# Splitting GpSimd's first load by partitions in a diagonal prefix-sum kernel

## The chip, the cores and the metric

The kernel runs on one core of a Trainium2 chip. The metric is the device time of one execution in microseconds; shown are the median and the extremes of three runs. One further execution was taken with the hardware profiler; all views of the profile are of that one.

## The reference

The input is four float32 matrices of 4224 x 4224. For each the two-dimensional prefix sum is formed, its diagonal is taken, and the diagonal is summed up again:

```python
def setup_inputs():
    B, H, W = 4, 4224, 4224
    return {"x": np.random.randn(B, H, W).astype(np.float32)}

def reference(x):
    ps = np.cumsum(np.cumsum(x, axis=1), axis=2)
    diag = np.diagonal(ps, axis1=1, axis2=2)
    return np.cumsum(diag, axis=1).astype(np.float32)
```

So the output has 4 x 4224 numbers, and every element of the input has to be read once: 285 MB.

## The kernel before

**Tiling.** A matrix is worked through in strips of 768 rows: partition p holds six consecutive rows of it, so a strip tile is 128 x 6 x 4224 in bfloat16 (6336 KB written, twice that read). Five such strips and one of 384 rows (three per partition) make a matrix; the last matrix (b = 3) ends in smaller pieces. The loads change float32 to bfloat16 on the way, which the loads issued from GpSimd do here. There are three strip buffers, reused in turn.

**What a strip needs.** `add_up` sums the columns right of the diagonal block with matmuls by the selector `sel` (lines 219 and 226), cuts the diagonal block with a mask (`tensor_mul` at 361, `tensor_sub` at 362), sums rows left of it on ACT (`act_sum`, 261) and on DVE (`row_sums`, 266). At the end of each matrix a few small operations on 11 x 384 numbers make its part of the output.

**Order.** The schedule is manual: each engine works in program order. DMAs go out on two queues: SyncE's (SP, line 78 and 83, and the results at the end), shown in the profile as q1 hardware_dynamic, and GpSimd's, shown as q0 software_dynamic, which carries all other loads. Both feed the same sixteen DMA engines. A load into a strip buffer (`load_rows`, line 71) waits for the buffer's earlier readers, and stands in GpSimd's order among GpSimd's other work.

**The start.** These steps stand ahead of everything else:

- line 78, SP: `opening`, row 0 of each partition's six in strip 0, in float32 (2112 KB), into the first strip buffer, used as float32 space
- line 83, SP: `head`, 128 x 2 x 528 numbers of the last matrix in float32 (528 KB)
- line 87, GpSimd: rows 1 and 2 of strip 0 (2112 KB written), then rows 3 to 5 (3168 KB), into the second buffer
- line 71, GpSimd: strip 1 (6336 KB) into the third buffer
- line 89, ACT: casts `opening` into row 0 of strip 0

Then, in program order: DVE sums `head` (line 93), makes `sel` (96, 97) and the first mask (102); GpSimd cuts the masks (103 and on) and makes some small constants up to line 208. GpSimd's next instruction after these is the load of strip 2 (line 71) into the buffer that `opening` held. Its wait is for SP's opening load and ACT's cast.

Of the kernel before, what the change touches and what calls it, by code (L numbers as in the profile page):

```python
# [17 lines left out]
def kernel(  # L18
# [14 lines left out]
    nc = tc.nc  # L33
# [3 lines left out]
    P = 128  # L37
    F = 3
    F2 = 2 * F
# [26 lines left out]
    def strip_tile():  # L66
        return strips.tile([P, F2, N], BF16, name="strip")

    def load_rows(o, b, r0):
        f = o.shape[1]  # L70
        nc.gpsimd.dma_start(  # L71
            out=o, in_=x[b, r0 : r0 + f * P, :].rearrange("(p f) w -> p f w", f=f)
        )


    src_0 = x[0, : F2 * P, :].rearrange("(p f) w -> p f w", f=F2)
# [6 lines left out]
    nc.sync.dma_start(out=head, in_=src_a[:, :, N - HC : N])  # L83

    prefetched = [strip_tile(), strip_tile()]
    for f0, f1 in ((1, F), (F, F2)):
        nc.gpsimd.dma_start(out=prefetched[0][:, f0:f1], in_=src_0[:, f0:f1])
    load_rows(prefetched[1], 0, F2 * P)
    nc.scalar.copy(out=prefetched[0][:, 0], in_=opening)  # L89

# [8 lines left out]
    def upper_mask(f):  # L99
# [22 lines left out]
        out=um1,  # L122
        in_=um1,
# [10 lines left out]
        out=ident,  # L134
        in_=ident,
# [32 lines left out]
    def between_groups(name, turned):  # L168
# [27 lines left out]
        out=weights,  # L196
        in_=weights,
# [12 lines left out]
        out=steps, in_=steps, scalar=2, op=ALU.arith_shift_right  # L210
# [112 lines left out]
    for b in range(B):  # L323
# [86 lines left out]
        for h in range(2):  # L410
# [3 lines left out]
                out=r6[ps, k : k + 2 * ns : 2, :], in_=a6[ps, :, :, 1]  # L414
# [27 lines left out]
        if not whole:  # L442
# [9 lines left out]
            for sb, c0, c1 in (  # L452
# [8 lines left out]
                    out=part_b[:, sb, c0:c1],  # L461
                    in_=x[b, r0 : r0 + R, :TB].rearrange("r (k c) -> r k c", k=4)[
                        :, :, c0:c1
                    ],
# [29 lines left out]
        for i, (to, src) in enumerate(((c1, d), (c2, c1))):  # L494
            nc.vector.tensor_tensor_scan(  # L495
                out=to,
# [52 lines left out]
        for i in (1, 0):  # L549
# [3 lines left out]
            out=out[b, T0 : T0 + M0].unsqueeze(0), in_=yl[:, :M0]  # L553
        )
        nc.sync.dma_start(
            out=out[:LB, :].rearrange("b (g i) -> g b i", i=GW), in_=whole_sums
        )
        nc.sync.dma_start(
            out=out[b, :T0].rearrange("(g i) -> g i", i=GW), in_=last_sums[1:NG]
# [3 lines left out]
        for i in (1, 0):  # L563
# [8 lines left out]
            out=out[b, T0 + M0 : T0 + E0].unsqueeze(0), in_=yl[:, M0:E0]  # L572
# [35 lines left out]
```

## Time and profile before

| | us |
|---|---|
| median of three runs | 667.44 (667.38 to 667.51) |
| the profiled execution's own time | 667.36 |
| its span, from first to last instruction | 665.6 |
| PE busy | 214.9 |
| DVE busy | 379.8 |
| ACT busy | 139.1 |
| POOL (GpSimd) busy | 31.6 |
| first GpSimd load: from issue to landing | 17.2 |
| opening load (SP): from issue to landing | 12.3 |
| head load (SP): from issue to landing | 38.9 |
| a six-row strip load: from issue to landing, median of 18 | 65.5 |

The span is cut into 40 equal slices for some rows; a digit is a busy share in tenths, and 9 stands for 90% or more. In the rows of DMA queues the three numbers are packets, MB (counted as written) and the share of the time of sixteen engines that the packets took; when packets overlap in the records, the share passes 100%. The chain of waits follows the work that ended last back from the end, and prints, for each piece, start and duration in us. In the timeline each row has start, duration, engine, line, operation, and in brackets how long the engine was idle before and what ended that.

### The profile page before, as it was taken

The page shows a single profiled execution, that of the slowest core. Times are in us where ns is not written, and L with a number is a line of the kernel's source. Part 1 is how long each engine was busy: PE and PEld are TensorE (multiplying, and loading weights), DVE is VectorE, ACT ScalarE, POOL GpSimd, SP SyncE. Part 2 cuts the span into 40 slices and gives each one's busy share as a digit, 9 for nine tenths or more (in the row PEclk, how much of TensorE's full clock was granted, in tenths as well). Part 3 has the DMA queues.
Part 4 walks back from the last instruction along what each step waited for, and adds up shares of the span by engine and source line. Part 5 has one row for each costly group of instructions (what it writes and reads, how often), then busy time and mean ns, then how long its engine had stood idle before and what let it go on. Part 6 is the DMA issues. An engine that isn't in the chain of part 4 may idle for free.

```text
span 665.6 us, 2565 instructions
## 1 busy us (share of the span) xinstructions
PE 214.9 (32%) x979; PEld 97.5 (15%) x980; DVE 379.8 (57%) x176; ACT 139.1 (21%) x220; POOL 31.6 (5%) x60
## 2 busy tenths in 40 slices
PE   0044522403118143140311723404031354340468
PEld 0021211100003021010000311201000121120123
DVE  0045938476946173756794526456589433362866
ACT  2001121406300103040630020304063002030433
POOL 1014000000000000000000000000000000001000
PEclk9996757556558585665655858667555595775768
DMA  9999999999999999999999999999999999999998
GB/s 256 223 227 219 219 219 219 213 207 215 219 219 218 219 220 219 218 218 213 210 218 219 217 216 219 219 219 214 218 213 215 220 213 219 218 219 218 218 204 162
DMA packets 7810, 144.31 MB, mean 217 GB/s; under 512 B 714, under 2 KB 1014, under 8 KB 2166
## 3 DMA queue, kind: packets, MB, share of 16 engines
q0 software_dynamic: 7312, 141.39, 99.2%
q1 hardware_dynamic: 486, 2.77, 1.2%
q8 instruction: 7, 0.11, 0.1%
q14 instruction: 5, 0.04, 0.0%
HBM read 285.47 MB, written 0.07 MB: 429 GB/s over the span
## 4 chain that ended last, share of the span: by engine, by line
DVE 47%; another core or an unknown queue 30%; DMA 18%; POOL 2%; issue 1%; PE 1%; DVEq 0%; SPq 0%; POOLq 0%
DVE acc L266 25%; DMA strip<-in_x_dram 12%; DVE rowed L266 7%; DVE mu L361 7%; DVE strip L362 7%; DMA head<-in_x_dram 6%; POOL um L103 1%; PE d L219 1%; DVE um L102 1%; DVE c L495 0%; DVE whole_sums L495 0%; POOL strip L460 0%; DVE pu L266 0%; DVE whole_sums L287 0%
## 5 line engine op out<-in xcount | busy, mean ns | idle before, releaser
L261 ACT ACTIVATE dump<-strip 128x416 bf16<-128x416 bf16 (+6 forms) x108 | 123.6, 1145 | 505.4 <-DMA strip<-in_x_dram 502.7
L266 DVE TENSOR_REDUCE acc<-strip 128x6 f32<-128x4608 bf16 (+6 forms) x23 | 195.9, 8518 | 0.4
L361 DVE TENSOR_TENSOR mu<-strip,um 128x4608 bf16<-128x4608 bf16 (+1 forms) x24 | 52.4, 2183 | 221.1 <-DMA strip<-in_x_dram 221.0
L226 PEld LDWEIGHTS <-sel 128*11 128x11 bf16 x643 | 66.5, 103 | 435.8 <-issue 406.1
L219 PE MATMUL d<-strip,sel 128*11 128x384 bf16 x90 | 36.5, 406 | 281.0 <-DMA strip<-in_x_dram 239.4
L226 PE MATMUL d<-strip,sel 128*11 128x384 bf16 x441 | 113.6, 400 | 0.0
L219 PE MATMUL d<-mu,sel 128*11 128x384 bf16 x43 | 16.6, 386 | 117.6 <-DVE mu L361 117.5
L362 DVE TENSOR_TENSOR strip<-strip,mu 128x4608 bf16<-128x4608 bf16 (+1 forms) x24 | 52.4, 2183 | 1.0
L266 DVE TENSOR_REDUCE rowed<-strip 128x384 f32<-128x2304 bf16 x12 | 48.8, 4067 | 0.0
L226 PE MATMUL d<-mu,sel 128*11 128x384 bf16 x200 | 48.0, 377 | 0.0
L71 POOL DMA_DIRECT2D strip<-in_x_dram x23 | 15.7, 681 | 500.7 <-DVE acc L266 268.2
L93 DVE TENSOR_REDUCE hs<-head 128x2 f32<-128x1056 f32 x1 | 1.3, 1253 | 40.2 <-DMA head<-in_x_dram 40.2
L219 PEld LDWEIGHTS <-sel 128*11 128x11 bf16 x134 | 13.6, 102 | 60.4 <-DVE sel L97 41.6
L219 PE MATMUL d<-rowed,sel_f 128*11 128x384 f32 x24 | 12.6, 616 | 25.3 <-DVE rowed L266 25.3
L261 ACT ACTIVATION_READ_ACCUMULATOR dump<-strip 128x1 f32 x108 | 20.1, 186 | 0.0
L219 PE MATMUL d<-ident,rows 128*11 128x128 f32 x24 | 5.2, 378 | 16.8 <-DVE rows L422 16.8
L219 PE MATMUL fold<-um,ident_h 128*128 128x512 bf16 x27 | 8.1, 475 | 0.3 <-issue 0.3
L103 POOL TENSOR_SCALAR_AFFINE_SELECT um<-um 128x4608 bf16<-128x4608 bf16 (+1 forms) x2 | 5.2, 2610 | 43.4 <-DVE um L102 43.4
L89 ACT CAST strip<-strip 128x4224 bf16<-128x4224 f32 x1 | 3.7, 3711 | 11.1 <-DMA strip<-in_x_dram 11.1
L219 PEld LDWEIGHTS d<-rowed,sel_f 128*11 128x11 f32 x24 | 1.4, 93 | 30.1 <-DVE rowed L266 30.0
L266 DVE TENSOR_REDUCE pu<-d 11x1 f32<-11x384 f32 x4 | 2.2, 546 | 6.2 <-PE d L219 6.2
L102 DVE MEMSET um<- 128x4608 bf16 (+1 forms) x2 | 4.9, 2458 | 1.1 <-issue 1.1
(108 smaller groups left out, 77.3 us busy)
## 6 DMA issues: line engine op xcount, KB each, us to landing
strip<-in_x_dram POOLq DMA_DIRECT2D x18, 6336.0 KB, 65.5
strip<-in_x_dram POOLq DMA_DIRECT2D x6, 3168.0 KB, 55.8
strip<-in_x_dram SPq DMA_DIRECT2D x1, 2112.0 KB, 12.3
strip<-in_x_dram POOLq DMA_DIRECT2D x1, 2112.0 KB, 17.2
strip<-in_x_dram POOLq DMA_DIRECT2D x1, 1080.0 KB, 49.9
strip<-in_x_dram POOLq DMA_DIRECT2D x1, 768.0 KB, 52.9
strip<-in_x_dram POOLq DMA_DIRECT2D x3, 256.0 KB, 54.1
head<-in_x_dram SPq DMA_DIRECT2D x1, 528.0 KB, 38.9
```

The lines of the kernel that those rows point to most:

```text
L71: nc.gpsimd.dma_start(out=o, in_=x[b, r0 : r0 + f * P, :].rearrange("(p f) w -> p f w", f=f))
L89: nc.scalar.copy(out=prefetched[0][:, 0], in_=opening)
L93: nc.vector.reduce_sum(out=hs[:, 0:2], in_=head, axis=AX.X)
L102: nc.vector.memset(um, 1.0)
L103: nc.gpsimd.affine_select(out=um, in_=um, compare_op=ALU.is_gt, fill=0.0, base=0, pattern=[[-1, f], [1, f * P]], channel_multiplier=-f,)
L219: nc.tensor.matmul(o, lhsT=lhsT, rhs=rhs, start=start, stop=False, skip_group_check=True)
L226: te.add_instruction(mybir.InstMatmult(start_tensor_calc=False, stop_tensor_calc=False, tile_position=(0, 0), tile_size=(P, P if lhsT.shap ...
L261: nc.scalar.activation(out=dump[:, :w], in_=src, func=ACT.Copy, accum_out=acc)
L266: nc.vector.reduce_sum(out=acc, in_=src, axis=AX.X)
L361: nc.vector.tensor_mul(out=mu, in0=block, in1=um)
L362: nc.vector.tensor_sub(out=block, in0=block, in1=mu)
```

## The change

GpSimd's first load, rows 1 and 2 of strip 0 for all 128 partitions, becomes two: the same rows for partitions 0 to 15, then for partitions 16 to 127. The load of rows 3 to 5 stays one. The same bytes go to the same places. All that follows on GpSimd, the other queue and the compute engines stand in the same order as before; line numbers behind it move by two. The consumers of strip 0, and the later load into its buffer, have one load more to wait for.

```diff
     prefetched = [strip_tile(), strip_tile()]
-    for f0, f1 in ((1, F), (F, F2)):
-        nc.gpsimd.dma_start(out=prefetched[0][:, f0:f1], in_=src_0[:, f0:f1])
+    for p0, p1, f0, f1 in ((0, 16, 1, F), (16, P, 1, F), (0, P, F, F2)):
+        nc.gpsimd.dma_start(
+            out=prefetched[0][p0:p1, f0:f1], in_=src_0[p0:p1, f0:f1]
+        )
     load_rows(prefetched[1], 0, F2 * P)
     nc.scalar.copy(out=prefetched[0][:, 0], in_=opening)
```

## The prediction

> **What bounds the kernel now.** I read the page from the whole to the start: first the slices and the queues, then the chain of waits at the end, then the first 60 us, where the change sits.
>
> ```profile
> span 665.6 us, 2565 instructions
> ...
> DMA  9999999999999999999999999999999999999998
> ...
> q0 software_dynamic: 7312, 141.39, 99.2%
> q1 hardware_dynamic: 486, 2.77, 1.2%
> ...
> HBM read 285.47 MB, written 0.07 MB: 429 GB/s over the span
> ```
>
> The DMA engines are above 90% busy in 39 of 40 slices, and the two queues together fill 100% of sixteen engines. DVE, the busiest compute engine, has 57%. So the time is the engines' work plus the little before and after it. The chain of waits from 600 us on says the same of the end:
>
> ```profile
> 607.03 11.74 another core or an unknown queue
> ...
> 619.06 43.20 DMA strip<-in_x_dram
> ```
>
> The last load lands at 619.06 + 43.20 = 662.26 us. After it come 3.3 us of sums and the write of the result. Whatever an engine loses earlier, it never wins back: it is busy until then.
>
> The start, in order of time:
>
> ```profile
> 0.82 0.41 SPq L78 DMA_DIRECT2D strip<-in_x_dram  x1
> 1.28 0.42 SPq L83 DMA_DIRECT2D head<-in_x_dram  x1
> 1.33 1.22 POOL L87 DMA_DIRECT2D strip<-in_x_dram  x2 [0.81 <-POOLq L592]
> 2.51 0.75 POOL L71 DMA_DIRECT2D strip<-in_x_dram  x1
> 13.18 3.71 ACT L89 CAST strip<-strip 128x4224 bf16<-128x4224 f32 x1 [11.09 <-DMA strip<-in_x_dram]
> ```
>
> SP's opening load (L78) goes out at 0.82 us, GpSimd's first load (L87) at 1.33 us. Four windows of the DMA view give the pace: the queues' packets, MB and share of sixteen engines for 1.85 to 5.5 us, 3.5 to 5.5 us, 5.4 to 6.0 us (here q0 appears) and 70 to 90 us.
>
> ```profile
> q1 hardware_dynamic: 80, 1.35, 101.9%
> ...
> q1 hardware_dynamic: 48, 0.81, 95.2%
> ...
> q0 software_dynamic: 16, 0.27, 210.8%
> ...
> q0 software_dynamic: 164, 4.16, 96.7%
> ```
>
> Before 1.75 us no packet moves. From 1.85 us SP's queue alone fills the engines (101.9%) until GpSimd's first sixteen packets start at 5.5 us. One packet of one engine takes share x window x 16 / packets: q1's 16,896 bytes 0.952 x 2.0 x 16 / 48 = 0.635 us; q0's 16,896 written bytes (two rows of one partition, twice that read) 2.108 x 0.6 x 16 / 16 = 1.265 us; the three-row packets of all later loads 0.967 x 20 x 16 / 164 = 1.887 us. q1's first round is slower: 80 packets are 5 to an engine, 5 x 0.744 - 4 x 0.635 = 1.18 us for the first.
>
> **The change, part by part.** *Earlier start.* GpSimd's first 16 partitions may be ready well before the 5.5 us at which all 128 were. But between 1.85 and 5.5 us the engines have no room: a q0 packet that starts earlier pushes a q1 packet back by the same time, and q1's 26 packets an engine must all run anyway. The work is the same bytes, so the gain is 0. A gain needs an idle engine; the only trace of one is the slow first round, 1.18 - 0.635 = 0.55 us, and q1 owns it. Between 0 and 0.55 I take 0.
>
> *One more issue on GpSimd.* L87's two issues took 573 and 652 ns, L460's five 528 to 578 ns: about 0.55 us, also for the small one. Everything behind it moves by that much: the issue of rows 3 to 5 and that of strip 1 (2.51 us). Their packets are needed only when the first load's end (landed 17.2 us after its issue) and at about 34 us (the 3168 KB load, 32.3 us after issue), so 14 us cover it. GpSimd's next work, L103, waits until 46.67 us for DVE. Later loads wait on the next semaphore of a ring of eight, each still on the same earlier load as before; the load into strip 0's buffer waits for three of them in place of two, and the waiting instruction's shortest row is 17 ns, hidden by the 15 us that GpSimd waits before it.
>
> *One more completion.* Each load ends with one 4-byte packet per engine; the sixteen of the opening load, in the window 12.4 to 12.9 us, fill 4.4% of sixteen engines: 0.044 x 0.5 x 16 / 16 = 0.022 us each. Cost 0.02 us.
>
> *A narrow load.* One packet on each engine now lands in 16 partitions in place of 128. No load of this trace does that. From below: the same bytes by the same queue take 1.265 us, cost 0. From above: the worst stretching in the trace is the first round's, 1.18 for 0.635, a factor of 1.86, which on 1.265 us is +1.09 us. Between them, the only transfers that touch few partitions are the results at the end (11 partitions read): 663.0 to 664.1 us holds 63 packets in 40.5%; less 23 completions at 0.022 these are (7.13 - 0.51) / 40 = 0.166 us for 1,536 bytes, 9.3 GB/s an engine, and 16,896 bytes at that pace take 1.82 us, +0.56. I take 0.55, as it is the only narrow row. All sixteen engines pay it once, at the start, and carry it to the end.
>
> [...]
>
> *Who takes turns.* The chain of waits to 60 us, and for the start to 40.2 us the two queues; strip 1's landing is in the same view:
>
> ```profile
> 1.28 38.86 DMA head<-in_x_dram
> 40.17 1.25 DVE hs L93
> 42.69 3.91 DVE um L102
> 46.67 5.17 POOL um L103 x2
> 57.00 38.33 DMA strip<-in_x_dram
> ```
>
> ```profile
> q0 software_dynamic: 352, 7.03, 81.5%
> q1 hardware_dynamic: 416, 2.70, 18.0%
> ...
> strip<-in_x_dram POOLq DMA_DIRECT2D x1, 6336.0 KB, 61.9
> ```
>
> DVE's first work waits for the small head load (L83); behind it stand the masks, GpSimd's masks and, after them, GpSimd's load of strip 2 (57.00 us). The head lands late because the queues take turns packet by packet: q1 sends 416 / 16 = 26 packets an engine (8 + 1 opening, 16 + 1 head), 80 / 16 = 5 of them alone, so 21 alternate with q0: 8 + 1, 8 + 1 and 3 of strip 1. With the change q0's order is 1 + 1, 7 + 1, 8 + 1, then strip 1. Entering at the same round, the extra completion fills a turn and the head lands 1.89 us earlier; for each round that q0 enters sooner, 1.89 us later. At most four rounds: 3 x 1.89 = 5.7 us, the head at 45.8.
>
> Strip 1 occupies the queue until 2.51 + 61.9 = 64.4 us. A load needs at most 5.5 - 1.33 = 4.2 us from issue to first packet (the only one seen on an empty queue), so strip 2 has 64.4 - 57.0 - 4.2 = 3.2 us to spare. DVE has more: it waits 9.97 us for strip 2 at 95.42. Cost 0 for up to three rounds less a little.
>
> **Sum.** 0 + 0 + 0.02 + 0.55 on the profiled run's own 667.36 us (span 665.6 and 1.76 around it): 667.93; with the runs' median of 667.44, 0.08 higher, about 668.0.
>
> **The rivals.**
> 1. *Nothing happens*: the narrow packets keep 1.265 us, or q0 comes no earlier. For it: equal bytes, engines full from 1.85 us. Against: narrow targets are unseen. 667.44 + 0.02 = 667.5.
> 2. *Strip 2's load comes too late* (slower). q0 enters right after q1's first round and keeps going, the head lands at 45.8, GpSimd issues strip 2 at 57.0 + 5.7 = 62.7, its packets come at 66.9, and the engines stand idle for 66.9 - 64.4 = 2.5 us: 667.44 + 0.02 + 2.5 = 670.0, or 670.5 with the narrow packets. It starts to cost when the head lands after 43.3, and passes 0.2% after 44.7. For it: the order of GpSimd's queue. Against: the other 112 partitions still need their time, and 4.2 us may be mostly a first use.
> 3. *A small gain*: q0 fills holes of the first round, at most 0.55: 666.9. Against: 101.9% share with q1 alone. More than that would need something this trace doesn't show.
>
> **How the numbers follow.** A measurement here tells about 0.2% (1.33 us) from no change. Forecast (narrow packets cost 0.3 to 1.1) 0.40, rival 1 0.30, rival 2 0.20, rival 3 0.10, half of it beyond what I can price. The first two and half the third are within 0.2%: 0.75, less 0.01 for a narrow load dearer than its bound, which would be slower. Faster 0.05, same 0.74, slower 0.21. The range runs from 666.9 (rival 3) to 669.4 (half of rival 2); outside are some 0.15.
>
> **What would show it.** In the profile after: a q0 group of sixteen packets before 5.5 us (its share over its number gives the narrow price: 1.265 us is rival 1, 1.8 the forecast); the first DVE row at 38 to 46 us; the DMA slices at 9 around 64 us, or a hole there for rival 2; the last landing later by just the narrow price. Wrong it would be if the sixteen engines got unequal shares of the 16 or the 112 partitions: each surplus packet adds 1.265 us to one engine, and the last engine sets the end.

## The result and the profile after

| | before | after |
|---|---|---|
| median, us | 667.45 (19 runs) | 668.55 (19 runs) |
| profiled execution's own time, us | 667.36 | 668.47 |
| its span, us | 665.6 | 666.8 |

The ratio is 1.0017, with a 95% interval of 1.0010 to 1.0023. So the kernel became 1.1 us slower, within the 0.2% that counts as no change here, but the sign is clear. Three of the 19 runs before took 668.5 to 668.6 us as well, for a reason that no trace here shows; the medians and the interval are over all runs.

First the page after, slices and queues as before:

```profile
span 666.8 us, 2568 instructions
...
DMA  9999999999999999999999999999999999999998
...
q0 software_dynamic: 7328, 141.39, 99.0%
q1 hardware_dynamic: 486, 2.77, 1.3%
...
HBM read 285.47 MB, written 0.07 MB: 428 GB/s over the span
```

GpSimd's queue has 16 packets more (7328 against 7312), the completions of the added load, and the same 141.39 MB. The engines are as full as before. The chain of waits at the end of the kernel after:

```profile
608.06 11.85 another core or an unknown queue
...
620.20 43.18 DMA strip<-in_x_dram
```

The last load lands at 663.38 us, 1.12 us later than before; what comes behind it takes 3.4 us, 3.3 before. The start of the kernel after, in the timeline:

```profile
0.81 0.40 SPq L78 DMA_DIRECT2D strip<-in_x_dram  x1
1.26 0.43 SPq L83 DMA_DIRECT2D head<-in_x_dram  x1
1.34 1.76 POOL L87 DMA_DIRECT2D strip<-in_x_dram  x3 [0.82 <-POOLq L594]
3.06 0.78 POOL L71 DMA_DIRECT2D strip<-in_x_dram  x1
13.18 3.71 ACT L91 CAST strip<-strip 128x4224 bf16<-128x4224 f32 x1 [11.09 <-DMA strip<-in_x_dram]
39.54 1.25 DVE L95 TENSOR_REDUCE hs<-head 128x2 f32<-128x1056 f32 x1 [39.54 <-DMA head<-in_x_dram]
```

The third issue costs GpSimd 1.76 - 1.22 = 0.54 us, and nothing waits for it. DVE starts 0.63 us sooner than before. Where the 1.1 us went in, the queues show in two windows of the kernel after, 5.4 to 6.2 us and 6.6 to 8.2 us (packets, MB, share of sixteen engines):

```profile
q0 software_dynamic: 16, 0.27, 167.1%
...
q1 hardware_dynamic: 16, 0.27, 103.4%
```

The first line is the round of narrow packets, one on each engine: 1.671 x 0.8 = 1.34 us each, little over the 1.265 us of a wide one. The second is the round right behind it, of SP's opening load: 1.034 x 1.6 = 1.65 us each. The same round of the kernel before, in the window 6.7 to 7.2 us:

```profile
q1 hardware_dynamic: 16, 0.27, 128.4%
```

1.284 x 0.5 = 0.64 us. So the delay is 0.07 us on the narrow packets and 1.01 us on the packets behind them, 1.08 us of the 1.10. GpSimd's first packets did not come sooner: in the records after there is one engine whose first one starts at 5.44 us, the fifteen others start between 5.60 and 6.19; before, the sixteen started between 5.54 and 5.92. In both kernels 80 packets of SP's, five to an engine, started first.

### The profile page after: what moved, and what is told of

Its sections match the earlier page's. It is cut to its first block, busy times and chain, and to the rows that moved or that the text cites. A ratio compares the mean times of both kernels' runs of the same rounds, so it can differ in the third digit from the quotient of the medians.

```text
span 666.8 us, 2568 instructions
## 1 busy us (share of the span) xinstructions
PE 211.5 (32%) x980; PEld 96.5 (14%) x980; DVE 380.1 (57%) x176; ACT 139.1 (21%) x220; POOL 32.0 (5%) x61
## 3 DMA queue, kind: packets, MB, share of 16 engines
q0 software_dynamic: 7328, 141.39, 99.0%
## 4 chain that ended last, share of the span: by engine, by line
DVE 47%; another core or an unknown queue 30%; DMA 18%; POOL 2%; issue 1%; PE 1%; DVEq 0%; SPq 0%; POOLq 0%
DVE acc L268 25%; DMA strip<-in_x_dram 12%; DVE rowed L268 7%; DVE mu L363 7%; DVE strip L364 6%; DMA head<-in_x_dram 6%; POOL um L105 1%; PE d L221 1%; DVE um L104 1%; DVE c L497 0%; DVE whole_sums L497 0%; DVE pu L268 0%; POOL strip L462 0%; DVE whole_sums L289 0%
```

## The experiments

All are variations of the kernel before. "Before" times are the runs beside them on the same chip; intervals are of the ratio to them.

**Is it the second load, or its narrowness?** Cut by rows in place of partitions, so that each load is 128 partitions wide:

```diff
-    for f0, f1 in ((1, F), (F, F2)):
+    for f0, f1 in ((1, 2), (2, F), (F, F2)):
```

> One load more as in the change, but cut by rows: row 1 and row 2 of strip 0 for all 128 partitions, no load narrow. If the 1.1 us of the change come from sixteen engines writing into 16 neighbouring partitions, this costs only the extra completion and smaller packets: 667.4 to 667.7. If a second load as such costs 1.1 us, 668.5.

Measured 667.62 beside 667.42, ratio 1.0005 (0.9997 to 1.0014). One load more, as in the change, and the median is 0.20 us higher; three of the eleven runs took 668.5. The interval of -0.2 to +0.9 us leaves out the change's 1.10 but not a smaller cost. The eight strided loads below are the sharper test: seven loads more, and the interval is -0.6 to +0.7 us for all of them together.

**How wide must it be?** The split at 32:

```diff
+    for p0, p1, f0, f1 in ((0, 32, 1, F), (32, P, 1, F), (0, P, F, F2)):
```

> The split put at partition 32 (32 and 96). Narrow-target theory, with the rate growing in proportion to the partitions reached: the first load's 32 packets need as long as two normal rounds (16 partitions stretched a round of 1.265 by about 1.1, 32 partitions give twice the rate, which is the normal one): 667.4 to 667.8. If any first load that is short costs 1.1 us, or two narrow rounds cost twice: 668.5 to 669.6.

Measured 667.48 beside 667.42, ratio 1.0002 (0.9993 to 1.0011). Its profile, SP's round right behind the first packets of the 32-partition load (window 6.6 to 7.4 us):

```profile
q1 hardware_dynamic: 16, 0.27, 80.2%
```

0.802 x 0.8 = 0.64 us, the undelayed value. With twice the partitions no cost is seen.

**Paid once or each time?** Two narrow loads, then the rest:

```diff
+    for p0, p1, f0, f1 in ((0, 16, 1, F), (16, 32, 1, F), (32, P, 1, F), (0, P, F, F2)):
```

> Two narrow loads (partitions 0 to 15, 16 to 31), then the other 96. Narrow-target theory: each narrow load costs its own 1.1 us, +2.2, 669.6 to 669.7. If the cost belongs to the very first GpSimd load (a start-up effect), +1.1 once: 668.5 to 668.6.

Measured 669.80 beside 667.42, ratio 1.0041 (1.0029 to 1.0054): +2.38, twice the change's cost. It is not a cost of the first load.

**Does it depend on its neighbours?** The narrow load second, behind the 112:

```diff
+    for p0, p1, f0, f1 in ((0, 112, 1, F), (112, P, 1, F), (0, P, F, F2)):
```

> The narrow load comes second: partitions 0 to 111, then 112 to 127. Narrow-target theory: the same +1.1 wherever it stands, 668.5. If the cost comes from the opening load's large float32 packets running beside it, or from being first, it falls to 0 to 0.3 here, as SP sends only small packets by then: 667.5 to 667.8.

Measured 668.27 beside 667.42, ratio 1.0012 (1.0003 to 1.0021): +0.85. The cost stays. The interval of +0.2 to +1.4 us can't tell 0.85 from 1.1, and the profiled run took 668.53, which is 1.1 more; the other expectation's 0 to 0.3 is met only by the lowest end of the interval. That SP's large packets are needed for the cost is excluded by the next run.

**Thirty microseconds later.** Strip 0 as before, and the load of strip 1 split instead:

```diff
-    load_rows(prefetched[1], 0, F2 * P)
+    src_1 = x[0, F2 * P : 2 * F2 * P, :].rearrange("(p f) w -> p f w", f=F2)
+    for p0, p1 in ((0, 16), (16, P)):
+        nc.gpsimd.dma_start(out=prefetched[1][p0:p1], in_=src_1[p0:p1])
```

> Strip 0 as before; the load of strip 1 (six rows a partition, two packets of 25,344 bytes an engine) is split at partition 16 instead. It runs 30 us later, with no large packets of SP beside it. Narrow-target theory: 811 KB into 16 partitions at the pace of the change (270 KB in 1.265 + 1.1 = 2.37 us, 114 GB/s) take 7.1 us in place of 3.8: +3.3, 670.8. A start-up effect: 667.4 to 667.6.

Measured 670.63 beside 667.44, ratio 1.0048 (1.0034 to 1.0062): +3.19 where 3.3 was worked out from the pace. In its profile, the window 36.3 to 37.2 us holds the second round of narrow packets:

```profile
q0 software_dynamic: 16, 0.41, 392.9%
q1 hardware_dynamic: 11, 0.02, 32.0%
```

3.929 x 0.9 = 3.54 us for a packet that elsewhere takes 1.887. SP's 2,112-byte packets between them are stretched as well, to 0.320 x 0.9 x 16 / 11 = 0.42 us; in the records of the kernel before they took 0.09 to 0.10.

**Sixteen partitions, or sixteen neighbours?** Rows 1 and 2 in eight loads of 16 partitions, in steps of eight and in blocks:

```diff
+    for p in range(8):
+        nc.gpsimd.dma_start(
+            out=prefetched[0][p:P:8, 1:F], in_=src_0[p:P:8, 1:F]
+        )
+    nc.gpsimd.dma_start(out=prefetched[0][:, F:F2], in_=src_0[:, F:F2])
```

> Rows 1 and 2 of strip 0 as eight loads of 16 partitions, each taking every eighth partition. If the partitions' place decides (neighbours share a way in), most of the cost is gone: 7 more loads at 0.02 to 0.04, 667.5 to 668.5. If 16 partitions as such are slow, 8 x 1.1: 676.

```diff
+    for p in range(0, P, 16):
+        nc.gpsimd.dma_start(
+            out=prefetched[0][p : p + 16, 1:F], in_=src_0[p : p + 16, 1:F]
+        )
+    nc.gpsimd.dma_start(out=prefetched[0][:, F:F2], in_=src_0[:, F:F2])
```

> The same eight loads of 16 partitions, but each of 16 neighbours. Narrow-target theory: 8 x 1.1 = 8.8: 676.2. If the cost is paid once, or is hidden by later loads, 668.5 or less.

In steps of eight: 667.39 beside 667.44, ratio 1.0001 (0.9991 to 1.0010). In blocks: 676.80 beside 667.44, ratio 1.0141 (1.0127 to 1.0155), +9.36 or 1.17 a load. The same number of loads, the same sizes, the same sixteen engines; only which partitions a load names differs, and with them which rows of the matrix it reads. SP's round behind the first narrow packets, first with steps of eight (window 6.75 to 7.4 us):

```profile
q1 hardware_dynamic: 16, 0.27, 98.8%
```

then in blocks (window 6.6 to 8.2 us):

```profile
q1 hardware_dynamic: 16, 0.27, 104.7%
```

0.988 x 0.65 = 0.64 us against 1.047 x 1.6 = 1.68 us. The last load of the run in blocks shows that nothing of it is won back:

```profile
627.90 43.35 DMA strip<-in_x_dram
```

It lands at 671.25 us, 8.99 us later than before.

A load of 16 neighbours also reads from a small stretch of the matrix: two of every six rows within 96. That this reading is what is slow was not tested by a run of its own, but the trace of the kernel before speaks against it. The 256 KB loads of line 460 each read 32 neighbouring rows and write them to all 128 partitions, in packets of 2,048 bytes. The window 658 to 659 us holds packets of two of these loads alone:

```profile
DMA packets 114, 0.20 MB, mean 205 GB/s; under 512 B 14, under 2 KB 14, under 8 KB 114
```

From a stretch of at most 64 rows they were written at 205 GB/s.

**One load fewer.** Rows 1 to 5 in one load:

```diff
+    nc.gpsimd.dma_start(out=prefetched[0][:, 1:F2], in_=src_0[:, 1:F2])
```

> One load fewer than before: rows 1 to 5 of strip 0 in one. If each load costs something of its own (up to 1.1), 666.3; if a wide load costs only its completion of 0.02, 667.4.

Measured 667.60 beside 667.44, ratio 1.0003 (0.9994 to 1.0012): no gain is seen. A saving of 1.1 us is outside the interval, one of up to 0.4 is not.

**When is GpSimd's first load ready?** SP's opening load and ACT's cast left out; GpSimd reads row 0 as well. The output is complete.

```diff
-    opening = strip_tile()[:, 0:2].rearrange("p f w -> p (f w)").bitcast(FP32)
-    nc.sync.dma_start(out=opening, in_=src_0[:, 0])
...
-    for f0, f1 in ((1, F), (F, F2)):
+    for f0, f1 in ((0, F), (F, F2)):
...
-    nc.scalar.copy(out=prefetched[0][:, 0], in_=opening)
```

> SP's opening load and ACT's cast are gone; GpSimd's first load takes rows 0 to 2 of all 128 partitions. SP sends only the 528 KB head, which is through after some 1.3 us, so the engines stand idle until GpSimd's first packet, and its start shows when that load is ready. If it was ready only at about 5.4 us: first packet at 5.4, some 2 us of idle engines, 669.5. If it had been ready at about 2.5 us and waited for its turn behind SP's packets: 667.4.

And the same with the split:

```diff
+    for p0, p1, f0, f1 in ((0, 16, 0, F), (16, P, 0, F), (0, P, F, F2)):
```

> As the run without the opening load, with GpSimd's first load split at partition 16 as in the change. If fewer partitions are ready sooner (the prediction's step), the first packet is earlier than in that run by up to 3 us. If the wait from issue to first packet doesn't depend on the size of the load, it starts at the same time. The narrow load of three rows (405 KB at 114 GB/s, 3.6 us for 1.9) then costs 1.7: 671.2 if that run is at 669.5.

Without the opening: 667.42 beside 667.41, ratio 0.9999 (0.9990 to 1.0008). With the split as well: 668.37, ratio 1.0015 (1.0006 to 1.0025), +0.95 over the run without it, where 1.7 was expected. The queues in the window 3.5 to 4.0 us, 128 partitions wide:

```profile
q0 software_dynamic: 11, 0.28, 261.5%
q1 hardware_dynamic: 84, 0.15, 79.7%
```

and split at 16:

```profile
q0 software_dynamic: 10, 0.25, 295.6%
q1 hardware_dynamic: 84, 0.16, 80.7%
```

In both no packet of GpSimd's moves before 3.5 us, and about two thirds of the engines have started on one by 4.0: the first at 3.67 us with 128 partitions and at 3.54 with 16, the last at 4.15 and 4.34. But in the records of both runs GpSimd's first packet starts, on each of the sixteen engines, as the last packet of SP's head ends there; from 3.5 to 4.0 us the DMA view counts 11 ends of the head (packets under 512 bytes) beside 11 of GpSimd's first packets, and 10 beside 10 with the split. The head was through between 3.5 and 4.3 us, later than expected, so the engines had no pause. The runs show that the load was ready by then, not since when, and can't tell whether 16 partitions are ready sooner than 128.

The loss of the split stands on the narrow packets and on those behind them, as in the change, though in other shares. GpSimd's first sixteen packets, in the window 3.5 to 4.5 us, with 128 partitions:

```profile
q0 software_dynamic: 16, 0.41, 189.8%
```

and with 16:

```profile
q0 software_dynamic: 16, 0.41, 248.5%
```

That is 1.90 us a packet against 2.49; in the records the sixteen packets behind take 2.35 us on average in place of 1.89. Together it is 1.05 us a pair of packets.

None of these versions beats the kernel before.

## Why the prediction was right

**The forecast's mechanism held, its size did not.** It said that narrow packets slow all sixteen engines once and that the loss stays to the end: +0.57, 668.0. It was +1.10. The term that was off is the narrow load: 0.55 us taken, 1.08 measured, just under the upper bound of 1.09 that came from the slow first round. That these two agree is chance: the bound was scaled from packets of SP's that go to all 128 partitions. I had scaled it from the results' packets, read from 11 partitions, which give 0.56. That row was the nearest by the number of partitions, but it reads SBUF, in small packets (1,536 bytes) with gaps between (a share of 40.5%); what neighbouring partitions do to a full stream of writes, it can't show.

From the runs the price can be worked out anew, as bytes over time, where the time is a normal round plus the loss: in the change 270 KB in 1.265 + 1.10 = 2.37 us, 114 GB/s; in blocks 2.16 MB in 8 x 1.265 + 9.36 = 19.5 us, 111 GB/s; in strip 1 811 KB in 2 x 1.887 + 3.19 = 6.96 us, 116 GB/s. Three sizes, nearly one pace (the run without the opening load, below, is the exception): sixteen neighbouring partitions take some 114 GB/s, against the 16 x 16,896 bytes / 1.265 us = 214 GB/s at which these loads write. If twice the partitions gave twice the pace, it would be 228 GB/s, just above that; this fits the run at 32, which shows no cost (667.48 us beside 667.42) but not the pace itself.

Of the cause the runs show that which sixteen partitions a load names decides, and with them which rows it reads: a load of sixteen neighbours cost 1.17 us in blocks, and eight loads of sixteen partitions in steps of eight cost nothing together, within -0.6 to +0.7 us. Why neighbours are slower no run shows.

**Where to look for the price** I had wrong in part: I expected the narrow group itself at 1.8 us a packet. It showed 1.34, and the delay stood on the packets of the other queue behind it, 1.65 us in place of 0.64. When the queues take turns, such a delay has to be summed over the narrow packets and those behind them.

**Earlier start: 0, but the premise was off.** The engines had no room, as I said (101.9% of them taken from 1.85 to 5.5 us), and the first packets came no sooner (from 5.60 to 6.19 us on fifteen of the engines, 5.54 to 5.92 before). I had taken 5.5 us as the time at which all 128 partitions were ready. With SP's opening load gone, a load of 128 partitions sent its first packet at 3.67 us, and then only as the head ended. If it is ready as early beside the opening load, at least 1.87 us of the wait until 5.54 were spent behind SP's packets. Whether 16 partitions are ready sooner stays open. The 4.2 us from issue to first packet, my bound for strip 2's load, was too long: in that run it was 3.67 - 1.32 = 2.35 us at most.

**One more issue and completion: hidden,** as worked out. 0.54 us on GpSimd, with 0.55 forecast.

**Turns of the queues.** The head was to land 1.89 us earlier if GpSimd's queue entered at the same round. DVE's first row moved from 40.17 to 39.54 us: 1.89 earlier by the turn, less 1.08 for the delay, gives 0.81; 0.63 was seen.

**The rivals.** *Nothing happens* is excluded by the interval. *Strip 2 too late* did not come about, as nothing entered earlier: GpSimd issued that load at 56.39 us, 0.61 before the old time. Its price was not tested. *A small gain* is excluded too. The upper end of the range, 669.4, was said to be half of rival 2; half of its 2.5 us on the forecast gives 669.2.

**What stays open:** why the narrow load of three rows, without the opening load, cost only +0.95, where 1.7 was expected. By the working above its pace is 143 GB/s. Counted in another way, from the start of the first narrow packet to the end of the last in the records, it is 405 KB in 3.86 us, 105 GB/s; the change has 99 GB/s by that count, and the split of strip 1 has 118. So the pace is known to some 15% by that count, and how the loss follows from it is not settled. Slow first packets don't explain the difference: GpSimd's first took 1.90 us without the split, where 1.887 is usual.

## What to carry to other kernels

Here the DMA engines were full almost from the first packet (101.9% from 1.85 to 5.5 us), and splitting a load gained nothing; the only question was what the pieces do to the engines' pace. Before a load is cut by partitions, compare what the partitions can take with what the engines send: 16 neighbours took some 114 GB/s of 214 here, and 32 neighbours or 16 spread ones showed no loss (667.48 us beside 667.42, 667.39 beside 667.44). If a small first piece is wanted, cut it by rows (667.62 us beside 667.42 here) or step over the partitions, and look for the cost of a narrow piece on the packets behind it, where 1.01 of 1.08 us stood in the change.

## What the runs showed of the hardware that was not expected

- **Turns did not start at once.** Beside SP's opening load GpSimd's first packet came at 5.54 us, after five of SP's packets on each engine, and from there the two queues alternated, a round of GpSimd's packets of 1.265 us and one of SP's of 0.64. Without the opening load the first came at 3.67 us, and on each engine only after all of SP's head. Why the turns begin where they do no run shows.
- **SP's opening load bought no time.** Without it, and without ACT's cast, the kernel took the same 667.42 us. The head, which had to take turns with packets of 1.265 and 1.887 us, then was used by DVE from 4.51 us on in place of 40.17, and the end did not move.
- **Extra loads in a full queue were free,** as long as they did not name neighbouring partitions alone: seven more, in steps of eight partitions, at 667.39 us, beside 667.44.
